# Attention, search, output projection and MLP of a hybrid trunk in two halves of the tokens

## The chip, the cores and the metric

The kernel runs on one core of one Trainium2 chip. Its engines are PE (TensorE, the matmuls, with PEld for their weight loads), DVE (VectorE), ACT (ScalarE), POOL (GpSimd) and SP (SyncE, which here only issues DMAs). Each engine takes its own instructions in order, and semaphores let them wait for each other. The metric is the device time of one execution in microseconds (us), the median of several.

## The reference

One transformer layer over 1,024 tokens of width 1,024, in float32:

```python
mod = silu(c) @ w_mod + b_mod                  # 6 vectors of 1,024: shift, scale, gate, twice
h = rmsnorm(x, g_attn) * (1 + sc1) + sh1
proj = h @ w_in                                # 1,024 -> 3,272 columns
o_a = stick_breaking_attention(q_a, k_a, v_a)  # 8 heads of 64, strictly causal
score = sum_j relu(q_idx_j . k_idx) * w_idx_j  # indexer, 8 heads; admissible: chunks of 64
_, idx = top_k(score, 256)                     # for each token
o_b = softmax(q . kv[idx] + bias) . kv[idx] . w_uv   # DSA attention, 8 heads, one latent of 128
o = concat(rmsnorm(o_a), rmsnorm(o_b))
x = x + ga1 * (o @ w_out)
h = rmsnorm(x, g_mlp) * (1 + sc2) + sh2
x = x + ga2 * (relu(h @ w_up) ** 2 @ w_down)   # 1,024 -> 4,096 -> 1,024
out = rmsnorm(x, g_final)
```

Stick-breaking weights are sigmoid(z) times the product of 1 - sigmoid(z) over the later admissible keys. A token sees no later chunk, so its attention needs keys and values up to its own chunk only.

## The kernel before, in words

Tokens are cut into eight blocks of 128, b = 0 to 7; block b attends to 128(b+1) keys. Pairs of blocks are numbered i = 0 to 3. Each float32 matmul is made of three (or two) matmuls of float32r halves: an operand is split into a rounded high part (`hi`) and the rest (`lo`), and `mm3` (L177) adds hi·hi, hi·lo and lo·hi. A split of a weight tile costs a DMA from SP, a copy on ACT (L173) and a subtraction on POOL (L174); `load_split` does it.

The program runs in this order. (1) x is normalised and transposed, the modulation's first two vectors are computed, and the indexer's scores `sc[b]` are made for b = 2 to 7 (L245 to L468). (2) For four pairs of heads, `sb_project` makes queries and keys (`qe`, `qo`, `ke`, `ko` and low parts, for all tokens, kept in SBUF), and `sb_weights` and `sb_finish` do the stick-breaking attention for the pairs i in the order SBO: scores on PE, two sigmoids on ACT (L707, L708), a product scan on DVE (L709), a product on POOL (L711), then in `av_pair` transposes on PE (L621, L623), their split by ACT and DVE or POOL (L626 to L632), and the weighted sum on PE (L644). Beside it runs the search: `topk_step` finds the 256th largest score bit by bit in 32 steps, for blocks 2 to 6 by counts on DVE (L503, L529) and for block 7 by a sign count on ACT (L552), and `topk_mask` writes the masks `mk[b]`. `dq_half` projects the DSA queries and stores them to DRAM; `mod_piece` computes the rest of the modulation on DVE (L400, L402). (3) `ds_weights` and `ds_finish` do the DSA attention for all four pairs of blocks, head by head. (4) `out_tile` does the output projection (`wo`, with all of w_out split in SBUF), the second norm, and `h2_pair` transposes and splits its result. (5) In pools of its own the MLP runs in eight groups of four: `up` for both halves of the tokens from one split of the weights, then `dn` for all eight blocks.

The lists MS, DQ and TK and the offsets PRI set after which step of the attention how much of the other work is put into the program. The framework then orders the instructions of each engine at compile time: a list scheduler takes the instruction that comes first in the program (shifted by `early`) among those that it believes ready, and so moves later work into idle time, as far as the tiles' buffers allow. SBUF tiles share tagged pools of fixed numbers of buffers, PSUM has eight banks: z 4, tr 3, av 1 up to the MLP, then p1 4 and p2 4.

## Time and profile before

| | us |
|---|---|
| median of 3 runs | 1626.39 (1625.78 to 1627.17) |
| the profiled execution's own time | 1625.42 |
| its span, first to last instruction | 1623.6 |
| mean granted PE clock, of full | 0.948 |
| PE busy | 1468.8 |
| DVE busy | 990.5 |
| ACT busy | 667.6 |
| POOL busy | 567.5 |

An engine's busy time is the time in which at least one of its instructions ran. Matmuls overlap in the records, since each is followed by the next before its own end, so that PE's busy time is longer than the time that the same matmuls need when they follow each other closely.

### The profile page before, as it was taken

Reading aid. Unit: us, or ns where it says so; the run is one execution under the profiler, and the core shown is the slowest. Engines: PE = TensorE matmul, PEld = TensorE weight load, DVE = VectorE, ACT = ScalarE, POOL = GpSimd, SP = SyncE. Lnnn points to the kernel's source line nnn. Section 1 sums busy time; section 2 is a strip of 40 time slices with the busy share of each in tenths; the row PEclk is TensorE's granted clock in tenths of the full one; section 3 lists DMA queues with packets and bytes.
Section 4 is the critical chain, followed back from the end, with each engine's and each line's share of the span. In section 5 each row is a group of like instructions: output and inputs, shape, how many; then the busy total and the mean of one; then the engine's idle time right before and its main releaser. Section 6 shows DMA issues by size and latency. Waiting matters only on the chain.

```text
span 1623.6 us, 19672 instructions
## 1 busy us (share of the span) xinstructions
PE 1468.8 (90%) x7248; PEld 1213.9 (75%) x7248; DVE 990.5 (61%) x1842; ACT 667.6 (41%) x1258; POOL 567.5 (35%) x389
## 2 busy tenths in 40 slices
...
PEclk8999979888899879999999999999999999999999
...
GB/s 324 150 105 28 78 46 39 105 64 91 34 40 40 68 55 85 91 59 53 117 143 101 208 94 0 92 13 78 26 65 40 53 52 39 66 27 78 6 34 104
DMA packets 103232, 121.49 MB, mean 75 GB/s; under 512 B 7856, under 2 KB 75480, under 8 KB 103136
## 3 DMA queue, kind: packets, MB, share of 16 engines
...
q14 instruction: 39, 0.32, 0.1%
...
## 4 chain that ended last, share of the span: by engine, by line
PE 61%; DVE 27%; issue 4%; ACT 3%; DMA 3%; POOL 1%; SPq 0%; DVEq 0%; POOLq 0%; ACTq 0%
PE up L178 7%; PE up L180 7%; PE up L179 7%; PE dn L178 7%; PE dn L179 7%; PE dn L180 7%; DVE tk_jk L503 4%; DVE tk_jk L529 4%; DVE m L709 4%; DVE m2acc L402 2%; DMA wm<-in_w_mod_dram 2%; PE wo L178 2%; PE wo L179 1%; PE wo L180 1%; PE avd L644 1%
## 5 line engine op out<-in xcount | busy, mean ns | idle before, releaser
L174 POOL TENSOR_TENSOR wld<-wrd,whd 128x1024 fp32r<-128x1024 f32 x32 | 77.3, 2415 | 474.5 <-ACT whd L173 474.5
L1138 DVE TENSOR_TENSOR x<-dn,x 128x512 f32<-128x512 f32 x128 | 87.7, 691 | 206.7 <-PE dn L180 206.7
L1119 ACT ACTIVATE r<-up 128x512 f32<-128x512 f32 x64 | 37.8, 591 | 402.7 <-PE up L180 402.7
L178 PE MATMUL up<-h2h,whup 128*128 128x512 f32 x512 | 200.0, 391 | 3.2 <-ACT h2f L1020 3.2
L179 PE MATMUL up<-h2l,whup 128*128 128x512 f32 x512 | 199.7, 390 | 0.0
L180 PE MATMUL up<-h2h,wlup 128*128 128x512 f32 x512 | 199.7, 390 | 0.0
L179 PE MATMUL dn<-wld,uh 128*128 128x512 f32 x512 | 199.2, 389 | 0.0
L180 PE MATMUL dn<-whd,ul 128*128 128x512 f32 x512 | 199.2, 389 | 0.0
L178 PE MATMUL dn<-whd,uh 128*128 128x512 f32 x512 | 196.6, 389 | 0.0
L1120 DVE SCALAR_TENSOR_TENSOR r<-up,r 128x512 f32<-128x512 f32 x64 | 44.3, 692 | 196.7 <-ACT r L1119 196.7
L711 POOL TENSOR_TENSOR be<-be,m 128x895 f32<-128x895 f32 (+7 forms) x64 | 89.5, 1401 | 170.0 <-DVE m L709 114.8
L709 DVE TENSOR_TENSOR_SCAN m<-m 128x896 f32<-128x896 f32 (+7 forms) x64 | 98.7, 1548 | 27.7 <-ACT m L707 25.3
L178 PEld LDWEIGHTS up<-h2h,whup 128*128 128x128 f32 x512 | 96.5, 188 | 23.5 <-ACT h2f L1020 3.5
L179 PEld LDWEIGHTS up<-h2l,whup 128*128 128x128 f32 x512 | 96.5, 189 | 20.1
L180 PEld LDWEIGHTS up<-h2h,wlup 128*128 128x128 f32 x512 | 96.4, 188 | 20.1
L178 PEld LDWEIGHTS dn<-whd,uh 128*128 128x128 f32 x512 | 96.1, 188 | 20.0
L180 PEld LDWEIGHTS dn<-whd,ul 128*128 128x128 f32 x512 | 96.1, 188 | 20.0
L179 PEld LDWEIGHTS dn<-wld,uh 128*128 128x128 f32 x512 | 96.1, 188 | 19.9
L174 POOL TENSOR_TENSOR wlup<-wrup,whup 128x1024 fp32r<-128x1024 f32 x32 | 77.1, 2408 | 27.3 <-ACT whup L173 27.2
L160 DVE TENSOR_TENSOR ul<-r,uh 128x512 fp32r<-128x512 f32 x64 | 57.2, 894 | 44.7 <-ACT uh L159 44.7
L529 DVE TENSOR_SCALAR_CACHE_REDUCE tk_jk<-mk,tlo,above 128x384 bf16<-128x384 uint16 (+4 forms) x80 | 74.7, 933 | 2.0
L644 PE MATMUL avs<-wts,va 128*128 128x256 f32 (+1 forms) x320 | 56.5, 306 | 16.4 <-DVE ota L662 7.3
...
## 6 DMA issues: line engine op xcount, KB each, us to landing
...
```

Source lines behind the costliest of these rows:

```text
L160: (lo_eng or V).tensor_tensor(lo, src, hi.bitcast(F32), op=OP.subtract)
L174: (lo_eng or G).tensor_tensor(lo, raw, hi.bitcast(F32), op=OP.subtract)
L178: T.matmul(ps, ah, bh, start=start, stop=False)
L179: T.matmul(ps, ah, bl, start=False, stop=False)
L180: T.matmul(ps, al, bh, start=False, stop=stop)
L503: V.tensor_scalar(jk[:, :widths[b]], src or sc[b], t, 0.5 - TOPK, op0=op, op1=OP.add, accum_out=c)
L529: V.tensor_scalar(jk[:, :widths[b]], mk[b].bitcast(U16), tlo[:, j:j + 1], above[:, j:j + 1], op0=OP.is_ge, op1=OP.add, accum_out=cnt[0][:, ...
L644: T.matmul(dst, vv, rhs, start=kt == 0 and l == 0, stop=half and l == 1)
L709: V.tensor_tensor_scan(m[:, :n][:, ::-1], m[:, :n][:, ::-1], m[:, :n][:, ::-1], 1.0, op0=OP.mult, op1=OP.bypass)
L711: G.tensor_tensor(be[:, :n - 1], be[:, :n - 1], m[:, 1:n], op=OP.mult)
L1120: V.scalar_tensor_tensor(r, ps, 0.0, r, op0=OP.max, op1=OP.mult)
L1138: V.tensor_tensor(x1[tt][:, cs], ps, x1[tt][:, cs], op=OP.add)
```

## The change

The tokens are worked in two halves of 512, hf = 0 (blocks 0 to 3) and hf = 1 (blocks 4 to 7), from the attentions to the end of the MLP. The projections are still made for all tokens, but q, k and v of the second half go to DRAM (`qd`, `khd`, `kld`, `vd`; the stores are issued by ACT) and come back head by head in `sb_second`. The search has two DVE groups, blocks (2, 3) and (4, 5, 6), beside block 7 on ACT. The first part of the program does stick-breaking and DSA attention of half 0, then `out_half(0)`. After that `mlp_beside` yields the MLP of half 0 in 96 steps (32 `up`, 64 `dn`), which the program alternates with stick-breaking of half 1, the rest of the search, and DSA of half 1. Then come `out_half(1)` and the MLP of half 1 alone. The weights w_up, w_down and w_out are therefore loaded and split once per half. What is left of the modulation after the indexer moves from DVE to ACT and POOL. The SBUF tiles qk, kl and va become one pool `qk` of 14 tiles of 4 KB. PSUM is z 3, tr 2, av 1 and a new m 2, which serves the projections and the MLP of half 0.

```diff
...
-TKB = ((2, 3, 4, 5, 6), (7,))
-TK0 = 1
...
+DEPTH = 2
+BUFS = {"wkL": 4, "wkS": 6, "qk": 14, "wt": 3, "ot": 2, "ot2": 1, "z": 4, "tr": 3, "av": 1}
+PS2 = {"z": 3, "tr": 2, "av": 1, "m": 2}
 MI = [4, 0, 5, 0, 2, 0, 0, 5]
-MS = [2, 0, 1, 2, 2, 1, 1, 1, 1, 1, 0, 1, 1, 0, 0, 0, 0, 0, 0, 0, 0, 0, 0, 0, 0, 0, 0, 0, 0, 0, 0, 0]
-DQ = [1, 1, 1, 1, 1, 2, 0, 2, 0, 1, 1, 1, 0, 0, 0, 0, 0, 0, 0, 0, 0, 0, 0, 1, 0, 0, 1, 0, 1, 0, 1, 0]
-TK = [1, 1, 2, 1, 1, 2, 0, 2, 2, 1, 4, 0, 4, 0, 2, 0, 1, 2, 4, 3, 0, 0, 1, 0, 2, 1, 1, 1, 0, 0, 0, 3]
+MS = [2, 2, 2, 2, 2, 2, 2, 2, 1, 1, 1, 1, 1, 1, 1, 1]
+DQ = [0, 0, 0, 0, 0, 0, 0, 0, 0, 0, 0, 0, 1, 1, 1, 1]
+TK = [3, 3, 3, 3, 3, 3, 3, 3, 3, 3, 3, 2, 0, 0, 0, 0]
+TA = [2, 2, 2, 2, 2, 2, 2, 2, 2, 2, 2, 2, 2, 2, 2, 2]
+D0 = [0, 1, 1, 2]
+FILL_S, FILL_T = 4, 3
+FILL_D = [2] * 18
 DBG = {}
...
+        def mtile(name):
+            return pp.tile([P, 512], F32, tag="m", bufs=bf["m"], name=name)
...
         def pjtile(name):
-            return pp.tile([P, 512], F32, tag="tr", bufs=TRB, name=name)
+            return (mtile if "m" in bf else trtile)(name)
...
-                if k == 0:
-                    V.tensor_scalar(acc, raw[:, 0, :], ck, None, op0=OP.mult)
+                if "m" in bf:
+                    A.activation(acc if k == 0 else raw[u], raw[u], AF.Copy, scale=ck)
+                    if k:
+                        G.tensor_tensor(acc, acc, raw[u], op=OP.add)
+                elif k == 0:
...
+        def search(blocks):
...
+                    V.tensor_tensor(thr, thi, fb, op=OP.bitwise_or)
+            yield begin
+            for i in range(31, 15, -1):
+                yield lambda i=i: upper_step(i)
+            for i in range(15, -1, -1):
+                yield lambda i=i: lower_step(i)
...
-                stack_q(ps, slice(hf * 512, hf * 512 + 512), r["qe"], r["qo"])
...
+                stack_q(ps, slice(0, 512), q[:, 0:512], q[:, 512:])
+                if hf:
+                    A.dma_start(qd[pr], q.bitcast(F32))
...
-                for k, l, p0 in ((r["ke"], r["le"], 0), (r["ko"], r["lo"], 64)):
...
                     p1 = 64 - p0
                     own, twin = slice(p0, p0 + 64), slice(p1, p1 + 64)
-                    A.activation(k[own, cs], ps[own], AF.Copy)
...
-                     lambda: (start_k(), half_k(0)), lambda: half_k(1)]
+                    A.activation(kl[own, 0:512], ps[own], AF.Copy)
+                    V.tensor_tensor(kl[own, 512:], ps[own], kl[own, 0:512].bitcast(F32), op=OP.subtract)
+                    if hf == 0:
+                        A.dma_start(kl.bitcast(F32)[twin, :], kl.bitcast(F32)[own, :])
+                        r[n] = kl
+                    A.dma_start(khd[pr][own, cs], kl.bitcast(F32)[own, 0:512])
+                    A.dma_start(kld[pr][own, cs], kl.bitcast(F32)[own, 512:])
...
+        def sb_weights(h, i, q, k, l):
             ws = []
+            if i < 2:
+                both = big(f"be{h}_{i}")
             for b in (2 * i, 2 * i + 1):
                 n = widths[b]
-                be = wktile(f"be{h}_{b}", n)
+                be = both[:, (b % 2) * 512:] if i < 2 else big(f"be{h}_{b}")
...
+        def sb_second():
...
+            def load(h):
+                pr, own = h // 2, slice(64 * (h % 2), 64 * (h % 2) + 64)
+                q = bp.tile([P, 512], F32R, tag="wkS", bufs=bf["wkS"], name=f"q2_{h}")
+                SY.dma_start(q.bitcast(F32), qd[pr][:, (h % 2) * 512:(h % 2 + 1) * 512])
+                kl = []
+                for n, src in (("h", khd), ("l", kld)):
+                    k = qktile(f"k2{n}_{h}")
+                    for p0 in (0, 64):
+                        SY.dma_start(k.bitcast(F32)[p0:p0 + 64, :], src[pr][own, :])
+                    kl.append(k)
+                v = qktile(f"v2_{h}").rearrange("p (k d) -> p k d", d=P)
+                SY.dma_start(v.bitcast(F32), vd[h // 4].rearrange("p (k h d) -> p k h d", h=4, d=P)[:, :, h % 4, :])
+                r[h] = (q, *kl), [v[:, k, :] for k in range(NB)]
...
+            def step(h, i):
+                if i == 3:
+                    if h % 2 == 0:
+                        ots[h // 2, 1] = bp.tile([P, 512], F32, tag="ot", bufs=bf["ot"], name=f"otc{h // 2}")
+                    if h < 7:
+                        load(h + 1)
+                todo.append((h, i, sb_weights(h, i, *r[h][0]), r[h][1]))
+                if len(todo) > 1:
+                    sb_finish(*todo.pop(0))
...
+        def vb_group(g, hf):
+            hi, lo = load_split([P, 4, 64], w_uv[4 * g:4 * g + 4].rearrange("h r d -> r h d"), f"u{g}_{hf}")
...
+        def ds_load(h, hf):
             r = {}
-            r["ql"] = qktile(f"dql{h}")
...
-            SY.dma_start(raw, dqd[h])
-            r["qh"] = qktile(f"dqh{h}")
+            raw = wktile(f"dqr{h}_{hf}", 512)
...
+            r["qh"], r["ql"] = both[:, 0:512], both[:, 512:]
             split(r["qh"], r["ql"], raw, A, G)
             if h % 2 == 0:
...
+        def ds_steps(hf):
+            todo = []
+            r = [None]
+            def first():
+                vb_group(0, hf)
+                r[0] = ds_load(0, hf)
+            def step(h, i):
+                todo.append((h, i, ds_weights(h, i, r[0])))
+                if i % 2 == 0:
+                    r[0] = ds_load(h + 1, hf) if h < 7 else None
+                if h == 3 and i % 2 == 0:
+                    while todo:
+                        ds_finish(*todo.pop(0))
+                    vb_group(1, hf)
+                if len(todo) > DEPTH:
+                    ds_finish(*todo.pop(0))
+            yield first
+            for h in range(8):
+                for i in (2 * hf + 1, 2 * hf):
+                    yield lambda h=h, i=i: step(h, i)
+            yield lambda: [ds_finish(*t) for t in todo]
+        pctx1.close()
+        bf.update(PS2)
+        pp = pctx.enter_context(tc.tile_pool(name="psb", bufs=1, space=PSUM, reuse_waits="tile"))
         r, steps = sb_project(0)
...
+        def wo_piece(kt, ch, hf, gate):
+            cs = slice(ch * 512, ch * 512 + 512)
+            n = f"o{hf}_{kt}_{ch}"
+            both = qktile(f"wb{n}")
+            hi, lo = both[:, 0:512], both[:, 512:]
+            load_halves(hi, lo, w_out[kt * P:(kt + 1) * P, cs], n, (bp, "wkS", bf["wkS"]), gate[ch])
+            return hi, lo
...
+        def out_half(hf):
...
+            zs = [(mtile if t == 3 else ztile)(f"wo{hf}_{t}") for t in range(4)]
+            for kt in range(KT):
+                hi, lo = wo_piece(kt, 0, hf, gate)
+                for t in range(4):
+                    ts = slice(t * P, (t + 1) * P)
+                    mm3(zs[t], oh_[kt, hf][:, ts], ol_[kt, hf][:, ts], hi, lo, kt == 0, kt == KT - 1)
+            w = [wo_piece(kt, 1, hf, gate) for kt in range(KT)]
...
+            for t in range(4):
+                ts = slice(t * P, (t + 1) * P)
+                xt, tt = xts[t], 4 * hf + t
+                z = ztile(f"wp{hf}_{t}")
+                for kt in range(KT):
+                    mm3(z, oh_[kt, hf][:, ts], ol_[kt, hf][:, ts], *w[kt], kt == 0, kt == KT - 1)
+                V.tensor_tensor(xt[:, 512:], z, xt[:, 512:], op=OP.add)
+                A.dma_start(x1d[tt * P:(tt + 1) * P, :], xt)
...
+        def up_tile(ft, hf, ps, r, uh, ul, lo_eng=None):
+            wuh, wul = load_split([P, KT, P], wu[:, :, ft * P:(ft + 1) * P], f"up{ft}_{hf}")
+            for kt in range(KT):
...
+        def mlp_beside():
...
+            def wd_load(fg, f, ch):
+                ft = fg * FFG + f
+                cs = slice(ch * 512, ch * 512 + 512)
+                both = qktile(f"wd{ft}_{ch}")
+                wd[f, ch] = both[:, 0:512], both[:, 512:]
+                load_halves(*wd[f, ch], w_down[ft * P:(ft + 1) * P, cs], f"d{ft}_{ch}", (bp, "wkS", bf["wkS"]))
+            def up(fg, f):
+                ft = fg * FFG + f
+                uh[f], ul[f] = htile(f"uh{ft}"), htile(f"ul{ft}")
+                up_tile(ft, 0, mtile(f"up{ft}"), wktile(f"r{ft}", 512), uh[f], ul[f])
+                wd_load(fg, f, 0)
...
+            def dn(fg, t, ch):
+                ps = mtile(f"dn{fg}_{t}_{ch}")
+                ts = slice(t * P, (t + 1) * P)
+                cs = slice(ch * 512, ch * 512 + 512)
+                for f in range(FFG):
+                    mm3(ps, uh[f][:, ts], ul[f][:, ts], *wd[f, ch], f == 0, f == FFG - 1)
...
+                else:
+                    V.tensor_tensor(acc[t, ch], ps, acc[t, ch], op=OP.add)
+                if ch == 0:
+                    wd_load(fg, t, 1)
...
+                    V.tensor_tensor(acc[t, ch], acc[t, ch], gate[0][ch], op=OP.mult)
+                    G.tensor_tensor(acc[t, ch], acc[t, ch], x1, op=OP.add)
...
+            for fg in range(NG):
+                for f in range(FFG):
+                    yield lambda fg=fg, f=f: up(fg, f)
+                for ch in range(2):
+                    for t in range(4):
+                        yield lambda fg=fg, t=t, ch=ch: dn(fg, t, ch)
+        norm(0, 0)
+        norm(0, 1)
+        run(s1, 1)
+        out_half(0)
+        run(s1, 1)
+        m = mlp_beside()
+        for _ in range(13):
+            run(s1, 1)
+            run(tk, FILL_T)
+            run(ta, 2)
+            run(m, FILL_S)
+        run(tk, 99)
+        run(ta, 99)
+        d = ds_steps(1)
+        for k in range(18):
+            run(d, 1)
+            run(m, FILL_D[k])
+        norm(1, 0)
+        run(m, 200)
+        norm(1, 1)
+        out_half(1)
+        pctx.close()
...
+        def up_group(fg):
             for f in range(FFG):
                 ft = fg * FFG + f
-                wuh, wul = load_split([P, KT, P], wu[:, :, ft * P:(ft + 1) * P], f"up{ft}")
-                uh[f] = gp.tile([P, S], F32R, tag="g4", bufs=16, name=f"uh{ft}")
-                ul[f] = gp.tile([P, S], F32R, tag="g4", bufs=16, name=f"ul{ft}")
-                for hf in (1, 0):
-                    cs = slice(hf * 512, hf * 512 + 512)
-                    ps = ptile(f"up{ft}_{hf}")
-                    for kt in range(KT):
-                        mm3(ps, wuh[:, kt, :], wul[:, kt, :], h2h[kt, hf], h2l[kt, hf], kt == 0, kt == KT - 1)
-                    r = gp.tile([P, 512], F32, tag="sq", bufs=2, name=f"r{ft}_{hf}")
...
```

## Rows read from the trace of the kernel before

**Rows 1.** The page: busy us, share and instructions of each engine; granted clock by slices.
```profile
PE 1468.8 (90%) x7248; PEld 1213.9 (75%) x7248; DVE 990.5 (61%) x1842; ACT 667.6 (41%) x1258; POOL 567.5 (35%) x389
...
PEclk8999979888899879999999999999999999999999
```

**Rows 2.** Windows by stage: length, busy us and instructions of PE, PEld, DVE, ACT, POOL, clock.
```profile
0.00:150.00 150.00, 113.50 (x542) 90.53 (x543) 119.41 (x168) 96.32 (x167) 59.73 (x51) 0.89 0.52 161
150.00:450.00 300.00, 240.39 (x1155) 194.85 (x1155) 294.58 (x620) 147.24 (x286) 95.04 (x60) 0.86 0.22 64
450.00:640.00 190.00, 159.06 (x910) 136.13 (x909) 134.66 (x141) 97.33 (x205) 102.97 (x64) 0.89 0.20 59
640.00:800.00 160.00, 149.01 (x1056) 128.25 (x1055) 144.09 (x492) 137.65 (x298) 100.68 (x72) 1.00 0.22 73
800.00:920.00 120.00, 110.33 (x526) 87.87 (x525) 59.50 (x118) 39.94 (x83) 50.55 (x56) 0.96 0.38 125
920.00:1617.00 697.00, 696.50 (x3070) 576.28 (x3068) 236.63 (x305) 148.41 (x220) 157.59 (x85) 1.00 0.18 57
```

**Rows 3.** Groups by line, PE: operation, shape, count, busy us, mean ns, idle before.
```profile
L178 PE MATMUL up<-h2h,whup 128*128 128x512 f32 x512 | 200.0, 391 | 3.2 <-ACT h2f L1020 3.2
...
L644 PE MATMUL avs<-wts,va 128*128 128x256 f32 (+1 forms) x320 | 56.5, 306 | 16.4 <-DVE ota L662 7.3 <-DVE wts L632 7.1 <-POOL wts L630 1.5
...
L178 PE MATMUL dq<-hh,whdq 128*128 128x512 f32 x128 | 54.8, 428 | 5.9 <-DVE qo L371 3.9 <-ACT whdq L173 1.3 <-ACT wfs L629 0.4
...
L623 PE MATMUL trs<-ident,be 128*128 128x128 f32 x160 | 41.0, 308 | 2.7 <-POOL be L711 2.7
...
L178 PE MATMUL v<-whv,hh 128*128 128x256 f32 x128 | 37.2, 290 | 0.0
```

**Rows 4.** Timeline of PE in the DSA stage: start us, us, operation.
```profile
769.36 0.27 PE L621 MATMUL trd<-ident,dl 128*128 128x128 f32 x1
769.47 0.27 PE L623 MATMUL trd<-ident,dl 128*128 128x128 f32 x1
...
770.99 1.13 PE L644 MATMUL avd<-wtd,vb 128*128 128x256 f32 x8
```

**Rows 5.** Groups by line, PE, window 640 to 800 us.
```profile
L644 PE MATMUL avd<-wtd,vb 128*128 128x256 f32 (+1 forms) x280 | 41.8, 286 | 2.6 <-DVE otb L662 1.1 <-ACT wtd L626 1.0 <-DVE wtd L632 0.3
L178 PE MATMUL dz<-kvh,dqh 128*128 128x384 f32 (+4 forms) x94 | 37.8, 403 | 4.2 <-DVE dst L812 3.0 <-DVE dst L817 1.1
```

**Rows 6.** Groups by line, DVE: scan, both kinds of count, modulation.
```profile
L709 DVE TENSOR_TENSOR_SCAN m<-m 128x896 f32<-128x896 f32 (+7 forms) x64 | 98.7, 1548 | 27.7 <-ACT m L707 25.3 <-POOL kvst L149 2.1
...
L529 DVE TENSOR_SCALAR_CACHE_REDUCE tk_jk<-mk,tlo,above 128x384 bf16<-128x384 uint16 (+4 forms) x80 | 74.7, 933 | 2.0
L503 DVE TENSOR_SCALAR_CACHE_REDUCE tk_jk<-mk,thr 128x384 bf16<-128x384 bf16 (+4 forms) x80 | 69.9, 874 | 1.2
...
L402 DVE SCALAR_TENSOR_TENSOR m2acc<-m2raw,c_act,m2acc 128x512 f32<-128x512 f32 x56 | 52.2, 932 | 7.5 <-DMA m2raw<-in_w_mod_dram 7.0
```

**Rows 7.** Groups by line, the MLP's work on the other engines.
```profile
L1138 DVE TENSOR_TENSOR x<-dn,x 128x512 f32<-128x512 f32 x128 | 87.7, 691 | 206.7 <-PE dn L180 206.7
...
L174 POOL TENSOR_TENSOR wlup<-wrup,whup 128x1024 fp32r<-128x1024 f32 x32 | 77.1, 2408 | 27.3 <-ACT whup L173 27.2
...
L160 DVE TENSOR_TENSOR ul<-r,uh 128x512 fp32r<-128x512 f32 x64 | 57.2, 894 | 44.7 <-ACT uh L159 44.7
...
L1120 DVE SCALAR_TENSOR_TENSOR r<-up,r 128x512 f32<-128x512 f32 x64 | 44.3, 692 | 196.7 <-ACT r L1119 196.7
...
L1119 ACT ACTIVATE r<-up 128x512 f32<-128x512 f32 x64 | 37.8, 591 | 402.7 <-PE up L180 402.7
```

**Rows 8.** Timeline of SP: one DMA issue.
```profile
702.61 0.32 SPq L831 DMA_DIRECT2D o<-otb  x1
```

**Rows 9.** Groups by form, DVE: the same comparison on 512 and 384 elements.
```profile
L578 DVE TENSOR_SCALAR eq<-sc,thr 128x512 f32<-128x512 f32 x1 | 1.7, 1696 | 0.0
...
L578 DVE TENSOR_SCALAR eq<-sc,thr 128x384 f32<-128x384 f32 x1 | 0.4, 395 | 0.0
```

849 lines of the change are left out of this document (392 added, 457 removed).

## The prediction, as put on record

> **What bounds the kernel now.** I read the page's busy times and clock first [rows 1], then the windows by stage [rows 2], then the groups by line, to count matmuls [rows 3, 5], and two timelines for spacings [rows 4, 8]. The reader is to see that PE is the busiest engine, but that its 90% is no measure of what it could give: in the last stage 3,070 matmuls of 512 columns start in 697.0 us, 0.227 us each, although each is recorded as 390 ns [rows 2, 3]. I therefore count work in spacings: 0.227 us for 512 columns; 0.12 us for 256 (eight in 1.13 us, the last of which ends some 0.3 us after its start) and 0.11 us for a 128-column transpose (769.36 to 769.47) [rows 4].
>
> In these units the work by stage is as follows, counts from the code and from [rows 3].
> - Projections: three lines of `mm3` with 128 matmuls each for dq, 384; as many for q and k together and for the output projection; kv 48. So q, k, dq and kv are 816 x 0.227 = 185 us, v (256 columns) 384 x 0.12 = 46, the output projection 384 x 0.227 = 87.
> - Stick-breaking: scores of 36 block columns of 128, twice, 8 heads, 144 times 512 columns, 33 us and 3 for the masks; 288 transposes 32; 320 weighted sums 38. Together 106 us.
> - DSA: scores three times instead of twice, 49 us and 3; transposes 32; sums 38; its values 48 x 0.12 = 6. Together 128 us.
> - Norms, the second transposes and the indexer's last pieces after 150 us: about 23 us.
>
> So from 150 to 920 us, 575 us of work took 770, three quarters. It splits unevenly. Between 640 and 800 us [rows 2, 5] ran 94/96 of the DSA scores, 7/8 of its sums and transposes, its values, and some 18 us of others: 51 + 33 + 30 + 6 + 18 = 138 of 160 us, 0.86, with DVE and ACT at 0.9. From 800 to 920 us about 100 of 120 ran. What remains, 575 - 138 - 100 = 337 us, took the 490 us from 150 to 640: 0.69. There DVE is full for 300 us (294.6) with the search's counts (145 us in all), the scans (99) and the modulation (52) [rows 6], and the granted clock is 0.86 to 0.89. The MLP's stage is bound by PE alone: 0.997, DVE at a third [rows 2]. Nothing can be won there, and some 150 us stand idle between 150 and 640.
>
> **The change part by part.** The stages after it are called A (to 150 us), B (projections, both attentions of half 0), C (output projection of half 0), D (MLP of half 0 beside the attentions of half 1), E (output projection of half 1), F (MLP of half 1).
>
> A: the same operations, 150 us.
>
> B: all projections, 185 + 46 = 231 us of PE. Of the attentions, blocks 0 to 3 have 1 + 2 + 3 + 4 = 10 of 36 block columns, 28%: 30 us and 36 us. With 15 for the spill from A and the small matmuls, 312 us. DVE has 32 counting steps for blocks 2 and 3: from the counts by width, 896 of 3,200 elements, 40 us, some 45 with small operations, masks and lower halves to 85; 28% of the scans and a little more since they are short, 33; the splits and evictions of projections and attentions, about 95; block 7's small operations 15. That is near 230 us. The rest of the search, about 135 us, is allowed to fill DVE's idle time here. The bounds of B are the two rates above: 312/0.86 = 363 and 312/0.69 = 452. I take 400, rate 0.78: less DVE work must be done here than before, but the filling counts again stand in front of other operations on an engine that takes them in order, and PE has only two banks for projections and two for transposes.
>
> C and E: 192 matmuls each, 44 us, and the gaps of such a chain (norm, square, power on POOL, transposes, split), 20 us in the row of 800 to 920 us [rows 2]. In C stick-breaking of half 1 is ready to fill, so I take 12 (0 to 20): 56. In E the last eight steps of the MLP cover the norm but not the way to the first `up`: 64.
>
> D: the MLP of half 0 is 1,536 x 0.227 = 349 us, stick-breaking of half 1 76, DSA of half 1 92: 517 us of PE. Done one after the other at the rates of before they take 349 + 76/0.69 + 92/0.86 = 566; perfectly mixed 517 to 520. I take 550, between them and nearer the first. DVE needs there about 71 (scans), 22 and 36 (splits of weights), 55 (DSA's sums and others), 95 for the MLP (32 x (692 + 894) + 64 x 691 ns [rows 7]) and 25 of masks, gates and last rows: some 305 us, and up to 440 if no count was done early. Both fit in 550.
>
> F: 349 us and the tail of 7 [rows 2]: 357 with a slower last pair.
>
> What is added and hidden: w_up and w_down are split twice. On POOL 32 x 2.41 us more for each [rows 7], 154 us, and 17 for w_out; POOL then has some 800 us over the program, about 310 in D, half of it. If PE didn't cover it, the 154 us would be the price. ACT gains some 70 us likewise. About 19 pieces of modulation move from DVE, 37 halves of 932 ns [rows 6], 34 us less, to ACT and POOL, which have room in B. The two search groups add 64 small operations: below nothing, above a count's own 874 ns each, 56 us; I take 16 us, on DVE, and it is in the 85 and 135 us. The round trip adds 74 DMA issues on ACT; at 0.32 us each as on SP [rows 8] 24 us of ACT in B, which also waits there in its order for the DVE half of each split, and behind it wait the next sigmoids and evictions; above, 74 times 1 us more. This is one reason why I don't put B at 0.86. The loads on SP are asked for a head ahead; SP's queue carries them past the MLP's weights, and a head has some 20 us of D, so I cost them at nothing.
>
> Sum: 150 + 400 + 56 + 550 + 64 + 357 = 1577. Outside the span lie 1625.42 - 1623.6 = 1.8 us, and the median of the runs is 1.0 above the profiled execution: 1580 us. Best bounds: 150 + 363 + 46 + 518 + 54 + 356 + 3 = 1490. Worst by the same rates: 150 + 452 + 64 + 566 + 70 + 358 + 3 = 1663.
>
> **The rivals.**
> First, better mixing: the list scheduler moves MLP matmuls into every gap, and B runs like the DSA stage. 150 + 363 + 50 + 522 + 60 + 357 + 3 = 1505. For it speaks that all engines but PE are under two thirds in D; against it, that before only one stage reached 0.86.
>
> Second, the other side, slower: the MLP's two `m` banks. Before, PE never waited for an eviction, with eight banks: DVE waited 206.7 us for `dn` [rows 7]. A `dn` step is 12 x 0.227 = 2.7 us, and its bank must be emptied by one DVE operation (691 ns) before the second next step; an `up` step needs ACT and DVE (591 + 692), and a group's first `dn` needs the whole chain with two more operations, about 2.8 us, behind whatever scan (up to 2.4) or mask stands in DVE's queue. If each of the 96 steps loses 1.2 us beyond what I allow, D is 665 and the time 1695; it decides from (1626 - 1580)/96 = 0.48 us a step. For it speaks that DVE and PE both take work in a fixed order that was planned at compile time; against it, that attention matmuls can stand between the steps.
>
> Third, no gain: B at 0.69, since the second search group keeps DVE full as in 150 to 450 us. 452 for 400 gives 1632.
>
> Fourth, DVE and POOL in turns. The rows show a comparison on 512 elements of 1,696 ns, where one on 384 takes 395 [rows 9], so something held it for a microsecond; but between 150 and 450 us DVE was busy 294.6 and POOL 95.0 of 300 [rows 2], so 90 us of POOL at least ran beside DVE. If POOL's 230 added us (the splits' 171 and the modulation's share) held DVE or were held in one to two thirds of the cases, and half of that came to light on PE, it is 40 to 75 us: up to 1655. The Trainium skill, "SBUF — State Buffer", section "Who interferes with whom", says that the two share one pair of ports as an exclusive lock, taken by DVE operations with two SBUF inputs or in a two-port mode; it speaks against a change that gives POOL 40% more to do, while counts with an accumulator are exempt. By that rule the scans' neighbours and the `ul` splits would meet POOL most, in D; the trace agrees with such single delays, and shows none as a rule.
>
> **How the numbers follow.** The forecast, 1545 to 1622, has 0.45; better mixing, 1485 to 1545, 0.17; no gain 0.13; the banks 0.17; the turns 0.08. Of "no gain" half lies within 0.2%, about what this kernel's measurement can tell from no change, and a little of it is faster. Faster: 0.45 + 0.17 + 0.02 = 0.64; same 0.06; slower 0.30. The range of 8 in 10 leaves the quickest twentieth and the worst of the banks' case: 1500 to 1675. The forecast's own range is 1545 to 1622.
>
> **What would show it.** In the changed profile: PE clock near 1.0 from C on; `up` and `dn` in two stretches, the later one some 350 us long at 0.227 us a matmul; the first `up` at about 610 us; counts of blocks 4 to 6 before that. D shorter than 566 us proves the mixing. The prediction is wrong if PE waits on DVE L1138's successor in `dn` for over 50 us, if B reaches past 620 us, or if the second stretch of the MLP starts late because its weights do.

## The result, and the profile of the changed kernel

The changed kernel takes 1735.6 us (median of 4 runs, 1733.6 to 1737.2) against 1626.8 for the kernel before on the same chip: ratio 1.0665, 95% interval 1.0646 to 1.0684. The forecast was 1580, the range ended at 1675. It is slower by 109 us, and 156 us above the forecast.

From the page of the changed kernel: PE's busy time and the granted clock in 40 slices. They answer to [rows 1].

```profile
PE 1512.3 (87%) x7352; PEld 1240.1 (71%) x7352; DVE 1101.0 (63%) x1943; ACT 776.4 (45%) x1414; POOL 783.9 (45%) x516
...
PEclk8989888999998797998899999999998899999999
```

The span is cut at the marks of the forecast's stages: the last weighted sum of DSA's first half (558 us), the first `up` (665), the last `dn` (1297), the first `vp` of the second MLP half (1377). Windows of the changed kernel by these marks (columns as in [rows 2], the last two numbers are the DMA engines' busy share and GB/s), and two stretches inside them:

```profile
0.00:150.00 150.00, 109.29 (x497) 83.91 (x498) 116.98 (x170) 96.96 (x171) 61.30 (x51) 0.89 0.52 164
150.00:558.00 408.00, 357.50 (x1942) 299.88 (x1943) 248.05 (x645) 223.98 (x443) 156.35 (x120) 0.92 0.40 115
558.00:665.00 107.00, 80.29 (x328) 61.87 (x328) 57.21 (x68) 41.62 (x78) 47.44 (x40) 0.80 0.37 114
665.00:1297.00 632.00, 560.96 (x2821) 462.14 (x2820) 441.43 (x827) 282.00 (x531) 305.21 (x189) 0.95 0.27 81
1297.00:1377.00 80.00, 53.86 (x234) 43.41 (x234) 49.65 (x65) 26.74 (x50) 42.05 (x42) 0.83 0.49 170
1377.00:1735.00 358.00, 350.37 (x1537) 288.94 (x1536) 187.65 (x171) 105.12 (x144) 171.53 (x76) 0.99 0.30 93
300.00:550.00 250.00, 233.86 (x1338) 197.56 (x1336) 104.45 (x259) 131.89 (x278) 102.55 (x81) 0.97 0.39 114
700.00:900.00 200.00, 153.19 (x691) 121.67 (x691) 196.18 (x331) 77.70 (x150) 84.04 (x49) 0.92 0.28 79
```

So A is 150 (forecast 150), B 408 (400), C 106 (56), D 632 (550), E 80 (64), F 358 (357). Three stages are right to within 8 us; the miss is C +50, D +82, E +16. (C ends at 664.5, hence 106.)

The last two windows show where D's loss sits. From 300 to 550 us DVE is busy 104 us of 250; from 700 to 900 it is busy 196 of 200, and PE 153. Groups of the changed kernel by line in that second stretch, with PE's wait at the end of its line:

```profile
L533 DVE TENSOR_SCALAR_CACHE_REDUCE tk_jk<-mk,tlo,above 128x640 bf16<-128x640 uint16 (+2 forms) x48 | 51.3, 1068 | 1.1
L502 DVE TENSOR_SCALAR_CACHE_REDUCE tk_jk<-mk,thr 128x640 bf16<-128x640 bf16 (+2 forms) x36 | 36.3, 1008 | 0.9
...
L158 PE MATMUL dn<-wd,uh 128*128 128x512 f32 x68 | 31.0, 463 | 19.6 <-DVE r L1131 17.2 <-DVE acc L1173 2.4
```

The two lines of counts are 84 of the 96 counts of the second search (blocks 4 to 6). Twelve were done before 665 us; the forecast had all of them in B's idle time. A timeline from the same stretch, cut down, shows what they stand in front of (start, duration, instruction):

```profile
864.75 2.41 POOL L155 TENSOR_TENSOR wlup<-wrup,whup 128x1024 fp32r<-128x1024 f32 x1 [0.99 <-ACT whup L154]
...
865.47 1.07 DVE L533 TENSOR_SCALAR_CACHE_REDUCE tk_jk<-mk,tlo,above 128x768 bf16<-128x768 uint16 x1
...
867.10 2.01 POOL L723 TENSOR_TENSOR be<-be,m 128x1023 f32<-128x1023 f32 x1
...
867.84 1.30 DVE L535 TENSOR_SCALAR cnt<-cnt 128x3 f32<-128x3 f32 x1
...
869.06 1.32 POOL L155 TENSOR_TENSOR wd<-wrd,wd 128x512 fp32r<-128x512 f32 x1
...
869.17 1.22 DVE L536 SCALAR_TENSOR_TENSOR tlo<-cnt,tlo 128x3 f32<-128x3 f32 x1
...
870.43 0.94 DVE L533 TENSOR_SCALAR_CACHE_REDUCE tk_jk<-mk,tlo,above 128x640 bf16<-128x640 uint16 x1
...
871.41 1.07 DVE L533 TENSOR_SCALAR_CACHE_REDUCE tk_jk<-mk,tlo,above 128x768 bf16<-128x768 uint16 x1
...
872.41 0.69 DVE L1131 SCALAR_TENSOR_TENSOR r<-up,r 128x512 f32<-128x512 f32 x1
...
873.15 0.50 PE L158 MATMUL up<-h2h,whup 128*128 128x512 f32 x1 [2.55 <-DVE r L1131]
...
874.25 0.17 DVE L535 TENSOR_SCALAR cnt<-cnt 128x3 f32<-128x3 f32 x1
```

PE stands for 2.55 us for a bank that one 0.69 us operation empties, because that operation is behind two counts and two small operations in DVE's order. The two small ones take 1.30 and 1.22 us here, while POOL works; the next of their kind, at 874.25 us with POOL idle, takes 0.17 (more on this in the last section).

### The profile page after: what moved, and what is told of

Read it like the earlier page. It is cut to its first block, busy times and chain, and to the rows that moved or that the text cites. A ratio compares the mean times of both kernels' runs of the same rounds, so it can differ in the third digit from the quotient of the medians.

```text
span 1735.0 us, 20688 instructions
## 1 busy us (share of the span) xinstructions
PE 1512.3 (87%) x7352; PEld 1240.1 (71%) x7352; DVE 1101.0 (63%) x1943; ACT 776.4 (45%) x1414; POOL 783.9 (45%) x516
## 4 chain that ended last, share of the span: by engine, by line
PE 54%; DVE 21%; POOL 5%; DMA 4%; issue 4%; ACT 3%; ACTq 0%; SPq 0%; POOLq 0%; DVEq 0%
DVE tk_jk L502 4%; PE en L158 3%; PE en L159 3%; PE en L160 3%; DVE m L721 3%; PE vp L158 3%; PE vp L159 3%; PE vp L160 3%; DVE tk_jk L533 3%; PE up L158 2%; PE dn L158 2%; PE up L159 2%; PE up L160 2%; PE dn L159 2%; PE dn L160 2%
## 5 line engine op out<-in xcount | busy, mean ns | idle before, releaser
L155 POOL TENSOR_TENSOR wlup<-wrup,whup 128x1024 fp32r<-128x1024 f32 x64 | 164.5, 2572 | 116.8 <-ACT whup L154 106.8
L158 PE MATMUL dn<-wd,uh 128*128 128x512 f32 x256 | 108.0, 427 | 23.4 <-DVE r L1131 17.2
L721 DVE TENSOR_TENSOR_SCAN m<-m 128x384 f32<-128x384 f32 (+3 forms) x64 | 102.0, 1600 | 24.6 <-ACT m L719 24.3
L159 PE MATMUL dn<-wd,uh 128*128 128x512 f32 x256 | 106.2, 416 | 2.3 <-POOL wd L155 2.3
L160 PE MATMUL dn<-wd,ul 128*128 128x512 f32 x256 | 104.8, 410 | 1.7 <-DVE ul L137 1.7
L160 PE MATMUL up<-h2h,wlup 128*128 128x512 f32 x256 | 102.5, 401 | 0.0
L158 PE MATMUL vp<-h2h,whup 128*128 128x512 f32 x256 | 100.5, 392 | 0.0
L158 PE MATMUL en<-whe,vh 128*128 128x512 f32 x256 | 99.7, 390 | 0.7 <-DVE x1b L1259 0.7
L160 PE MATMUL vp<-h2h,wlup 128*128 128x512 f32 x256 | 100.2, 391 | 0.0
L159 PE MATMUL vp<-h2l,whup 128*128 128x512 f32 x256 | 100.2, 391 | 0.0
L159 PE MATMUL en<-wle,vh 128*128 128x512 f32 x256 | 99.6, 389 | 0.0
L160 PE MATMUL en<-whe,vl 128*128 128x512 f32 x256 | 98.8, 389 | 0.0
L153 DVE TENSOR_TENSOR wre<-wre,gate 128x1024 f32<-128x1024 f32 x32 | 76.7, 2396 | 18.3 <-DMA wre<-in_w_down_dram 18.2
```

Source lines behind the costliest of these rows:

```text
L153: V.tensor_tensor(raw, raw, scale, op=OP.mult)
L155: (lo_eng or G).tensor_tensor(lo, raw, hi.bitcast(F32), op=OP.subtract)
L158: T.matmul(ps, ah, bh, start=start, stop=False)
L159: T.matmul(ps, ah, bl, start=False, stop=False)
L160: T.matmul(ps, al, bh, start=False, stop=stop)
L721: V.tensor_tensor_scan(m[:, :n][:, ::-1], m[:, :n][:, ::-1], m[:, :n][:, ::-1], 1.0, op0=OP.mult, op1=OP.bypass)
```

## The experiments

All stages of all runs, in us, cut at the same marks. A is 150 everywhere. The ratio is to the kernel before on the same chip, with its 95% interval.

| run | B | C | D | E | F | median us | ratio |
|---|---|---|---|---|---|---|---|
| forecast | 400 | 56 | 550 | 64 | 357 | 1580 | |
| changed kernel | 408 | 106 | 632 | 80 | 358 | 1735.6 | 1.0665 (1.0646 to 1.0684) |
| e1_mask_last | 455 | 106 | 573 | 81 | 359 | 1727.4 | 1.0611 (1.0594 to 1.0628) |
| e2_no_second_search | 397 | 107 | 571 | 80 | 359 | 1667.7 | 1.0255 (1.0232 to 1.0277) |
| e3_third_bank | 411 | 108 | 627 | 90 | 358 | 1745.5 | 1.0724 (1.0708 to 1.0740) |
| e4_gate_at_sum | 405 | 99 | 633 | 78 | 357 | 1726.5 | 1.0609 (1.0585 to 1.0632) |
| e5_counts_spread | 442 | 106 | 569 | 82 | 358 | 1710.1 | 1.0529 (1.0510 to 1.0549) |
| e56_rows_elsewhere | 437 | 102 | 575 | 81 | 365 | 1713.9 | 1.0555 (1.0527 to 1.0583) |
| e56c_fill_first_projection | 442 | 177 | 528 | 82 | 365 | 1744.0 | 1.0733 (1.0716 to 1.0750) |
| e57_mlp_tail_last | 445 | 106 | D and E 647 | | 363 | 1711.6 | 1.0530 (1.0513 to 1.0546) |
| e8_counts_thin | 410 | 114 | 605 | 81 | 359 | 1719.6 | 1.0557 (1.0526 to 1.0587) |
| e89_dq_earlier | 438 | 109 | 603 | 80 | 358 | 1740.6 | 1.0692 (1.0663 to 1.0720) |
| e84_thin_gate_at_sum | 411 | 106 | 604 | 78 | 360 | 1711.8 | 1.0514 (1.0483 to 1.0546) |
| e11_pieces_split_before | 428 | 98 | 607 | 62 | 360 | 1707.6 | 1.0489 (1.0465 to 1.0513) |
| e2_11_no_counts_no_pieces | 424 | 99 | 581 | 63 | 358 | 1674.9 | 1.0284 (1.0248 to 1.0319) |
| e5_11_spread_pieces | 464 | 93 | 575 | 62 | 358 | 1705.0 | 1.0479 (1.0457 to 1.0501) |
| e12_11_block6_on_scalare | 433 | 102 | 592 | 64 | 360 | 1702.6 | 1.0459 (1.0435 to 1.0484) |
| e15_projection_undisturbed | 400 | 74 | 645 | 83 | 358 | 1710.0 | 1.0506 (1.0478 to 1.0534) |
| e16_all_together | 441 | 74 | 594 | 78 | 360 | 1701.7 | 1.0457 (1.0426 to 1.0487) |
| e13_attention_then_mlp | 458 | in the text | | 87 | 357 | 1838.4 | 1.1297 (1.1272 to 1.1322) |

### Where the counts went

The first theory came from the code. Every count writes its unused output into one tile (tag `jk`, one buffer), tiles of a tag are given out in program order, and `run(ta, 2)` in the MLP's loop issues the mask of block 7 as its first thing, ahead of most of the second search. The rows on the tile `thr` of the changed kernel (first and last start at the end) agree: block 7's threshold stands at 287.5 us, its mask starts at 692.9.

```profile
L574 DVE TENSOR_SCALAR thr<-thr x1: 154/154/154, 287.5 to 287.5; 128x1 f32<-128x1 f32 x1
L575 DVE TENSOR_SCALAR nq<-sc,thr x1: 753/753/753, 692.9 to 692.9; 128x1024 f32<-128x1024 f32 x1
```

**e1_mask_last**

```
             run(s1, 1)
             run(tk, FILL_T)
-            run(ta, 2)
             run(m, FILL_S)
```

> One line goes: the mask of block 7 is no longer written into the MLP's loop but after the second search. First theory, the order of one 2 KB tile: every count of the search writes its unused result into one single tile, and such tiles are given out in program order. The mask of block 7 stands in that order ahead of all but the first three steps of the second search, and needs 4 KB tiles that are not free before the output projection is done; so the counts of blocks 4 to 6 can't move into the 60% idle time of VectorE between 300 and 550 us, and fill VectorE from 700 to 900 us, where PE does 131 us of work in 200. Then this run has those counts before 550 us, VectorE under 60% between 700 and 900, the MLP stage beside the attentions (668 to 1290 us now, 622 us) at 550 to 570 us, and 1660 to 1690 us in all. Second theory, the two banks of the MLP and the hand-over of its steps: the stage stays above 605 us and the time above 1715. Third, the counts are as much in the way before 550 us as later: the stage shortens, but the projections' stage grows by as much, 1725 to 1745.

**e2_no_second_search** (the counts of blocks 4 to 6 are left out; their masks use a threshold of zero)

```
-        tk, ta = chain(*[search(g) for g in GROUPS]), search_act(ACT_BLOCK)
+        tk, ta = chain(search(GROUPS[0]), search_none(GROUPS[1])), search_act(ACT_BLOCK)
```

> Leaves out the counts of the second search (blocks 4 to 6 get a mask with a threshold of zero), all else as in the changed kernel, the mask of block 7 in its place. It measures what those counts cost wherever they stand. First theory (their pile-up between 700 and 900 us): the MLP stage falls from 622 to 545 to 570 us and the time to 1655 to 1685. Second theory (banks and hand-over): the stage stays above 600 us, the time above 1710. If the run is well below the one with the mask moved, the counts cost something before 550 us too.

The windows 300 to 550 and 700 to 900 us of e1_mask_last, then the MLP stage of e2_no_second_search:

```profile
300.00:550.00 250.00, 207.90 (x1095) 172.41 (x1094) 188.73 (x432) 105.21 (x218) 89.04 (x70) 0.90 0.29 87
700.00:900.00 200.00, 185.50 (x927) 153.05 (x928) 104.73 (x111) 110.56 (x214) 126.44 (x75) 0.93 0.41 115
```

```profile
654.00:1225.00 571.00, 541.34 (x2823) 450.91 (x2821) 320.47 (x571) 282.59 (x532) 314.45 (x189) 0.98 0.30 90
```

One line moved the counts, as the first theory said: DVE from 300 to 550 us goes from 104 to 189 us, D from 632 to 573. But B pays 47 us for it, and the whole gains 8. All counts together cost 68 us (1735.6 - 1667.7) in the place that the change gave them, and 60 in e1's. So the first theory is right on where the loss of D comes from and wrong on what could be had; the third, "as much in the way before 550 us", holds. Of the 61 us between D with and without counts, 41 are idle time of PE (632 - 561 against 571 - 541), the other 20 its longer busy time at a lower granted clock (0.95 against 0.98).

**e3_third_bank**

```
-PS2 = {"z": 3, "tr": 2, "av": 1, "m": 2}
+PS2 = {"z": 2, "tr": 2, "av": 1, "m": 3}
...
-            zs = [(mtile if t == 3 else ztile)(f"wo{hf}_{t}") for t in range(4)]
+            zs = [(mtile if t >= 2 else ztile)(f"wo{hf}_{t}") for t in range(4)]
```

> The MLP gets a third PSUM bank and the scores one less (2 for 3). Second theory (two banks: a step must be emptied before the second next): PE waits less for the MLP's evictions, the stage of 622 us loses 30 to 60 us, 1675 to 1705 us. First theory (a full VectorE in order): the evictions are late by more than a bank can cover, and scores lose a bank: 1725 to 1750 us.

It is 10 us slower (E 90, D 627), as the first theory had it; the scores' lost bank is in that. Waits of PE in D, of the changed kernel and then of this run (total us, times, longest):

```profile
PE dn L158 <- DVE r L1131: 17.2, 6, 6.7
PE avs L660 <- DVE wts L648: 15.9, 10, 3.4
PE up L158 <- DVE r L1131: 8.4, 5, 2.6
PE dn L158 <- DVE acc L1173: 6.1, 5, 2.1
```

```profile
PE dn L158 <- ACT uh L136: 9.1, 2, 7.6
PE dn L160 <- DVE ul L137: 8.6, 5, 3.9
...
PE dn L158 <- DVE r L1131: 4.4, 4, 2.6
```

L1131 is the last operation that reads an `up` bank and L1173 the one that empties a `dn` bank, so in the changed kernel PE waits 32 us in D for the MLP's two banks (17.2 + 8.4 + 6.1). With three, `dn` waits 4 us for L1131 and 18 for its split inputs, which come later in the same order of DVE. And with two banks but without the counts, in e2, the waits for the banks are 6 us. So more banks don't help an eviction that stands behind counts.

**e5_counts_spread**, two search steps behind each eviction of a dq projection, held there by one copied element:

```
                 A.activation(f, ps, AF.Copy, scale=P ** -0.5)
+                jk = mp.tile([P, S], BF16, tag="jk", bufs=1, name=f"tk_jt{h}_{hf}")
+                V.tensor_copy(jk[0:1, 0:1], f[0:1, 0:1])
+                run(tk, 2)
```

with e1's line left out too.

> The mask of block 7 comes after the search as in the run that moved it, and two steps of the second search follow each of the 16 evictions of a dq projection; one copied element of that eviction, written into the search's single 2 KB tile, keeps them from being taken earlier. Before: moving the mask alone took 59 us off the MLP stage (632 to 573, from the first up to the last dn) and put 47 on the projections' (408 to 455), and the counts together cost 68 us wherever they stood, as the run without them showed. Theory of the bunch: the counts cost PE because some 25 us-long stretches of them stand back to back on an engine that takes its work in order; two steps (some 5 us) in each 10 us, where VectorE is idle for 60%, cost little: projections' stage 408 to 420, MLP stage 570 to 580, 1670 to 1690 us in all. Rival: every count is in front of something, so the price is the same anywhere: 1718 to 1735 us.

**e8_counts_thin**, one step at a time, in three stages (`count_after` is the copy and `run(tk, n)` of above):

```
                 ws.append(l)
+            if i < 2:
+                count_after(ws[-1], 1)
...
                 A.dma_start(x1d[tt * P:(tt + 1) * P, :], xt)
+                if hf == 0:
+                    count_after(xt, 1)
...
+                r = wktile(f"r{ft}", 512)
+                up_tile(ft, 0, mtile(f"up{ft}"), r, uh[f], ul[f])
+                count_after(r, 1)
```

> The second search one step (three counts, 4.4 us of VectorE) at a time, each behind a copied element of something late: 16 in the DSA of the first half (400 to 560 us), 4 in the first output projection, the rest behind one up step of the MLP each. The run with two steps behind each dq eviction still paid 42 us for the counts (1710 against 1668 without them), 34 of them in the projections' stage, where VectorE was full from 400 to 600 us. Theory of the bunch: one step in 10 us leaves VectorE idle between them, the projections' stage is 410 to 425 us, the first projection's 106 to 112, the MLP's 575 to 590: 1675 to 1695. Rival, each step costs its price wherever it stands: 1705 to 1730.

Spread counts cost 42 us, thin ones 52. The 16 steps that stand one per DSA step add 13 us to B (410 against 397 without counts), so bunching is part of the price; but the 12 steps left for the MLP's stage cost 34 us there (605 against 571), 2.8 us each for 4.9 us of DVE (379 us busy in the stage against 320). Unbunching takes off 26 of the 68 us at best, not the whole; both theories that put these runs at 1670 to 1695 were wrong, e8 lies in its rival's range and e5 below its own.

**e89_dq_earlier**

```
-DQ = [0, 0, 0, 0, 0, 0, 0, 0, 0, 0, 0, 0, 1, 1, 1, 1]
+DQ = [2, 0, 2, 0, 2, 0, 2, 0, 2, 0, 0, 0, 2, 0, 2, 0]
```

> The thin counts, and the dq projections no longer all behind the others (from 380 us on) but a head's two at every second step of the first attention, in the stretch from 200 to 300 us where PE does 31 us of work in 50 because VectorE is full of the first search. dq needs no VectorE. Theory (the projections' stage loses its time to what VectorE holds up, and PE has nothing else there): the stage of 408 us falls by 20 to 40 us, the rest as in the run with the thin counts. Rival: the two banks of the projections are given out in order, so that a dq step stands behind one whose bank waits for VectorE: within 8 us of the thin counts alone.

Neither: 21 us more. PE did take the work earlier (the last dq at 498 us, not 539), but then DSA and its thin counts stood alone at the end of B (from 500 to 560 us DVE is busy 58.8 us and PE 41.8, in e8 42.9 and 53.1), and the stage grew from 410 to 438. The dq matmuls had been the filler of that stretch.

### Whether the mixing is worth anything

**e13_attention_then_mlp** (based on e1's order of the mask)

```
-            run(ta, 2)
-            run(m, FILL_S)
...
             run(d, 1)
-            run(m, FILL_D[k])
+        run(m, 200)
         norm(1, 0)
-        run(m, 200)
```

> The mixing undone and nothing else: stick-breaking of the second half with the second search, then its DSA, and only then the MLP of the first half, all in the order of the program. One after the other at the rates of before I had 566 us for the three, mixed 550, and measured 632 with the counts in it and 571 without. If the mixing is worth what it seemed (PE takes MLP work where the attention waits): the stage from the first norm's end to the last dn is 80 to 130 us longer (counts and scans alone need 250 us of VectorE, DSA 110, the MLP 350), 1800 to 1860 us in all. If the mixing gives back what it wins by standing in VectorE's order: within 25 us of 1736.

Windows of this run, from the end of the first output projection to the first `up`, and from there to the last `dn`:

```profile
701.00:943.00 242.00, 164.36 (x842) 131.72 (x842) 169.99 (x256) 127.47 (x263) 98.66 (x68) 0.74 0.21 58
943.00:1392.00 449.00, 428.68 (x1991) 345.16 (x1990) 166.11 (x330) 161.57 (x273) 207.24 (x125) 0.99 0.29 89
```

The kernel with the mask moved and everything mixed takes 1727.4, this one 1838.4: the mixing is worth at least 111 us. At least, since the scheduler still put most of the DSA beside the MLP: 160 of its 224 weighted sums lie in the second window. Done nearly one after the other, the three parts take 691 us where the prediction had 566. The size that it had wrong is stick-breaking's: alone, and with no counts left to do (the last starts at 449.7 us), it and the rest of the DSA take 242 us at a granted clock of 0.74 with PE busy 68%, where the prediction's rate of 0.69 gave 110 for all of stick-breaking.

### The two projection stages

**e4_gate_at_sum**

```
-            load_halves(hi, lo, w_out[kt * P:(kt + 1) * P, cs], n, (bp, "wkS", bf["wkS"]), gate[ch])
+            load_halves(hi, lo, w_out[kt * P:(kt + 1) * P, cs], n, (bp, "wkS", bf["wkS"]))
...
+                V.tensor_tensor(g, z, gate[ch], op=OP.mult)
+                V.tensor_tensor(dst, g, dst, op=OP.add)
```

> In the two output projections the gate is no longer multiplied into the 16 pieces of the weights but into the 8 sums, as one more operation each. It is for the 115 and 90 us of the two projection stages (56 and 64 foretold). Theory of the pieces: each piece goes load, gate on VectorE, copy on ScalarE, difference on GpSimd through two free 2 KB tiles, 2.6 + 0.7 + 0.6 + 1.3 us and the waits between, one piece per 3 us; and the loads wait for the two gate tiles, which wait for the same small tiles. Without the gate the first piece comes some 15 us earlier and pieces follow every 2.2 us: the first stage falls by 15 to 30 us, the second by 5 to 15, 1690 to 1715 us in all. Rival: what holds the stage is that nothing of it can begin before the attentions of the first half free their tiles (548 to 583 us, PE at a third), and the way behind the last sum (norm, transposes, split); then the time falls by less than 10 us.

9 us, just the rival's side: C 99, E 78. **e84_thin_gate_at_sum** is the same edit on e8.

> The thin counts and the gate at the sums of the output projections. Alone the gate gave 9 us (7 in the first projection's stage, 2 in the second's). If the two are independent: 9 us less than the thin counts alone, 5 to 14. If the gate's gain came from VectorE in the MLP stage's pile-up: 0 to 4.

8 us less than e8 (C 106 for 114, E 78 for 81): independent of the counts.

**e11_pieces_split_before**, on top of e84; one call for each of the 16 steps of the first attention, and the projections load `wod`:

```
+        def wo_split(kt, ch):
+            both = big(f"ws{kt}_{ch}", F32R)
+            load_halves(both[:, 0:512], both[:, 512:], w_out[kt * P:(kt + 1) * P, ch * 512:ch * 512 + 512], f"o{kt}_{ch}", (bp, "wkS", bf["wkS"]))
+            A.dma_start(wod[kt, ch], both.bitcast(F32))
```

> The thin counts, the gate at the sums, and w_out split once, piece by piece during the first attention, both halves of each piece written to DRAM; the two output projections load them ready made, without the 2 KB tiles, ScalarE and GpSimd. It takes the chain of the pieces out of both projection stages (106 and 80 us). Theory of the pieces: the first sum starts some 15 us after the last weighted sum of the first half, in place of 36, and the stage falls to 70 to 85 us, the second to 62 to 72: 25 to 45 us less than with the gate alone. Rival, the chain of norms, transposes and free 4 KB tiles sets both stages: within 10 us of the run with the gate at the sums, or more, if 16 pieces more on ScalarE and GpSimd hold up the attention: the projections' stage then grows by 10 to 20.

4 us less than e84: which the runs' spread can't tell from nothing (1705.9 to 1709.0 against 1707.2 to 1715.5). By stages E falls to 62 as the theory of the pieces had it, C only to 98, and B grows by 17: the rival, within 10 us, holds for the sum. The second projection stage of this run:

```profile
1282.00:1344.00 62.00, 45.83 (x205) 36.87 (x203) 31.53 (x51) 16.07 (x31) 15.57 (x24) 0.86 0.53 199
```

So E was long because of its pieces, C for the most part was not, and the split costs in B most of what it gives.

**e56_rows_elsewhere** (x rows in idle tiles of the weights' pool, on e5) and **e56c_fill_first_projection** (eight steps of stick-breaking inside the projection):

```
-                xt = big(f"xr{hf}_{t}")
+                xt = wp.tile([P, S], F32, tag=("wh", "wl")[t // 2], bufs=2, name=f"xr{hf}_{t}")
```

```
+                fill()
+                fill()
                 if t % 2:
                     h2_pair(2 * hf + t // 2, xts[t - 1:t + 1])
...
-        out_half(0)
+        out_half(0, lambda: run(s1, 1))
```

> The spread counts, and the rows of x of the output projections no longer in the four 4 KB tiles that stick-breaking uses too, but in tiles of the weights' pool, idle there. Theory of the shared tiles (stick-breaking of the second half was to fill the output projection's stage, but the four x rows hold all four of its tiles from 590 us until the norm): the stage of 106 us keeps its length or loses up to 10, but stick-breaking steps run in it; 10 to 20 us less than with spread counts alone. Rival (the stage's own chain sets it, and the scores have no PSUM bank in it, since the sums hold three of three): within 6 us of it.

> As the run with the rows elsewhere, and two of the four sums in the MLP's banks, so that one bank is left for scores, and eight steps of stick-breaking written into the second part of the first output projection; the MLP's steps are dealt over the fewer steps that remain beside it. Theory of the shared tiles and banks: the 60 us in which PE stands in that stage take up to 38 us of scores, transposes and sums, the MLP stage falls by 20 to 35 us, 20 to 35 us less than with spread counts alone. Rival, DVE, ScalarE and GpSimd are then as late for the projection's own pieces as they were idle: the stage grows by what the MLP stage loses, within 8 us of spread counts alone.

The first gives nothing (1713.9 against 1710.1), the rival's case. The second went past both expectations: D falls by 41, more than its theory had, but C grows by 71. That was the hint: in C the filler is the trouble.

**e15_projection_undisturbed**, on the changed kernel

```
-        run(s1, 3)
+        run(s1, 1)
...
         norm(0, 1)
-        run(s1, 1)
         out_half(0)
-        run(s1, 1)
...
-        for _ in range(13):
-            run(s1, 1)
+        for k in range(13):
+            run(s1, 2 if k < 4 else 1)
```

> The changed kernel, and no stick-breaking of the second half ahead of or in the first output projection: its first four steps go into the MLP's loop (two a turn there at first). It was to fill that stage; the trace shows scans, products and sigmoids of it between 565 and 597 us, and the loads of the gates, of the x rows and of the first pieces of w_out waiting for its tiles (first piece asked for at 583 us, 25 after the last weighted sum). If the filler is what lengthens the stage: the first sum starts 15 to 25 us after the last weighted sum for 36, the stage is 72 to 88 for 106; the MLP stage gets 19 us of PE work more, which it does partly beside: 1705 to 1728 us in all. If the stage's own chain of norm, pieces and transposes sets it: 98 or more, and 1738 to 1755.

SP's timeline in this stage, of the changed kernel first, then of this run; between them what SP waited for in the changed kernel from 556 to 630 us:

```profile
562.21 15.69 SPq L1025 DMA_DIRECT2D gate<-gate  x2
583.52 0.33 SPq L151 DMA_DIRECT2D wro<-in_w_out_dram  x1
...
590.06 0.33 SPq L151 DMA_DIRECT2D wro<-in_w_out_dram  x1
...
596.33 31.72 SPq L151 DMA_DIRECT2D wro<-in_w_out_dram  x14
```

```profile
SPq L1025 <- PE sz L363: 15.1, 1, 15.1
SPq L151 <- POOL wts L646: 6.3, 2, 5.5
SPq L1095 <- PE trs L639: 5.1, 1, 5.1
...
SPq L1095 <- POOL be L723: 4.2, 1, 4.2
```

```profile
548.12 1.36 SPq L1025 DMA_DIRECT2D gate<-gate  x2
549.52 35.43 SPq L151 DMA_DIRECT2D wro<-in_w_out_dram  x16
```

```profile
150.00:550.00 400.00, 353.46 (x1941) 296.71 (x1940) 248.53 (x646) 223.73 (x443) 157.40 (x121) 0.94 0.39 116
550.00:625.00 75.00, 58.66 (x245) 47.40 (x246) 42.48 (x54) 26.10 (x45) 36.13 (x31) 0.84 0.39 121
625.00:1269.00 644.00, 571.91 (x2901) 471.80 (x2902) 460.20 (x839) 296.26 (x563) 323.88 (x197) 0.95 0.29 85
```

In the changed kernel all four waits end with an operation of stick-breaking (scores `sz`, transposes `trs`, `wts`, `be`), which lets go of the tile that the gate, the first piece or a row of x is loaded into. With stick-breaking kept out, the gates and the first piece are asked for at the end of the attention and not 25 us after it, the first sum starts 10 us after the last weighted sum (before, 35), C is 74 and the kernel 25.6 us faster, although D takes the four steps back with 13 us.

**e57_mlp_tail_last** (`run(m, 200)` behind `out_half(1)`, on e5)

> The spread counts, and in the second output projection's stage (80 us, foretold 64) the last steps of the MLP are written after the projection, so that they can fill its gaps instead of going ahead of it. Theory: PE waits there because the pieces of the weights get their small tiles only after the MLP's last rows (x1, y) have left them; with the order turned the first piece is loaded earlier and the eight steps of 2.7 us fill the gaps before the projection and before the next up: 10 to 22 us less than with spread counts alone. Rival: the two gates and the pieces still get no tile earlier and the chain stays: within 5 us, or up to 10 us more, since the MLP of the second half can't begin until the last rows are out.

Within 2 us of e5: the projection does start earlier (1247 us for 1284), and the last `dn` ends 79 us later (1345 for 1266), just before the second MLP half begins; D and E together are 647 for 651.

### Together

**e2_11_no_counts_no_pieces** joins the edits of e2 and e11 (again without the counts of blocks 4 to 6), **e5_11_spread_pieces** those of e5 and e11.

> Leaves out the counts of the second search (a threshold of zero for blocks 4 to 6), and has the pieces of w_out split before and the gate at the sums. Alone the counts were worth 68 us and, beside thin counts, pieces and gate together 12 (projection stages 114 to 98 and 81 to 62, but 18 more in the stage in which they are split). If the terms are independent: projections' stage 400 to 415, first projection's 92 to 100, MLP's 565 to 575, second projection's 60 to 65: 1640 to 1655 us, still above the kernel before; what is missing to the forecast then lies in the first projection's stage (40 us), in the MLP's (20) and in the projections' (10). If the MLP stage or the first projection's shrinks too (below 550, below 80), they waited for what was left out.

> Two steps of the second search behind each dq eviction (1710 us) with the gate at the sums and the pieces of w_out split before. The second projection's stage has 62 for 82, the first's 98 for 106, and 10 to 18 come back on the projections' stage: 1692 to 1706 us. It is the best order of the counts together with the best of the pieces. If the split of the pieces meets the counts on VectorE and GpSimd: 1706 to 1720.

Without counts the pieces are no gain at all (1674.9 against 1667.7: B +27, C -8, D +10, E -17), with spread counts 5 us. The terms are not independent: work put into B lengthens B.

**e12_11_block6_on_scalare**, on e11 (`run(ta, 2)` also goes beside each DSA step of the first half)

```
-GROUPS = ((2, 3), (4, 5, 6))
+GROUPS = ((2, 3), (4, 5))
...
-        tk, ta = chain(*[search(g) for g in GROUPS]), search_act(ACT_BLOCK)
+        tk, ta = chain(*[search(g) for g in GROUPS]), chain(search_act(ACT_BLOCK), search_act(6))
```

> The thin counts with the pieces split before (1708 us), and block 6, the widest of the second search, searched on ScalarE as block 7 is, after it: 32 signs with a sum and 64 small operations for VectorE in place of 32 counts of 896 elements. VectorE loses some 25 us of counts and gets 64 small operations of 0.15 us and more. Theory of VectorE's order (what stands in its queue is what PE waits for): the MLP stage of 607 falls by 10 to 25, 1680 to 1698 us in all. Rival: the small operations are as much in the way as the counts, or ScalarE gets late for the scores: 1700 to 1725.

D falls by 15, as the theory had it, but B and C take back 9 and E 2; 5 us less in all, inside the rival's range.

**e16_all_together** (e5, e4, block 6 on ScalarE, e15)

> What helped, together: two steps of the second search behind each dq eviction, block 6 on ScalarE, the gate at the sums, the first output projection undisturbed. Singly they gave 26, about 5 (beside other edits), 9 and what the undisturbed projection gives. If they add up: 1670 to 1695. If they meet in VectorE's order before 550 us: 1695 to 1715. No theory brings it below the 1627 of the kernel before.

1701.7, no clearer than e12's 1702.6, and 4.6% slower than the kernel before. C keeps its 74 us, but B is 441 and D 594 (569 in e5): the gains don't add up.

## Why the prediction was wrong, point by point

**A** and **F** came within 1 us. **B**'s 408 for 400 is luck: the 400, at the assumed mean of two rates, had the counts of blocks 4 to 6 in it, and the changed kernel did 12 of those 96 there. With the counts where the forecast put them (e1) B is 455, just past its worst bound of 452; without any (e2) it is 397. The costs of [rows 7]: the sums (L1173) 687 ns, as before; the split of w_up 2,572 ns where it took 2,408; w_down's gate 2,396 ns where it took 1,226 in the kernel before. None of it shows in F, where PE covers it. (The last stage's busy share is 0.999 by [rows 2], not 0.997; nothing hangs on it.)

```profile
L1173 DVE TENSOR_TENSOR acc<-dn,acc 128x512 f32<-128x512 f32 x56 | 38.1, 687 | 43.8 <-PE dn L160 43.8
```

```profile
L155 POOL TENSOR_TENSOR wlup<-wrup,whup 128x1024 fp32r<-128x1024 f32 x64 | 164.5, 2572 | 116.8 <-ACT whup L154 106.8
...
L153 DVE TENSOR_TENSOR wre<-wre,gate 128x1024 f32<-128x1024 f32 x32 | 76.7, 2396 | 18.3 <-DMA wre<-in_w_down_dram 18.2
```

**D: the step that failed is one sentence of B**, "The rest of the search, about 135 us, is allowed to fill DVE's idle time here". Nothing in the data forbids it; the order of a single scratch tile does, through the mask of a block that had been searched 400 us earlier. And the step left next to nothing for these counts: between B's 363 at the best rate and the 400 taken lie 37 us, which B without any of them used up (397). The fallback, "up to 440 if no count was done early. Both fit in 550", summed DVE over the stage. DVE's sum was exact (441 us), but the program deals the steps of the search over the turns of stick-breaking, ahead of the DSA that reads its masks, so they fell into 200 us, where DVE was full. That makes 61 of D's 82 us, and the runs say more: the work was never hideable for nothing, since no order brought its price below 42 us. The other 21 (571 without any count) are the term itself: its "one after the other" bound of 566 was far off (691), by 76/0.69 for stick-breaking, so that mixing gains at least 111 us where I had 16, and still doesn't reach 550. What makes up the 21 no run took apart.

**C: "In C stick-breaking of half 1 is ready to fill, so I take 12"** had the sign wrong. The filler holds the 2 KB and 4 KB tiles that the projection's loads wait for (SP's waits above), and its own operations stand on the engines that make the projection's splits. Together this is 32 of the 50 us, shown by leaving the filler out of the stage; the two were not told apart, except that moving the 4 KB rows of x alone gained nothing (e56). Some 18 us more than foretold remain in the undisturbed stage; its own chain of norm, pieces and transposes is what is left there, but no run took it apart.

**E**: the pieces of w_out had no term. With them ready E is 62 for 64 foretold, so the missing term is their way through load, gate, copy and difference: 18 us, of which the gate is 2 (e4). In the changed kernel the first sum of E starts 17 us after the last `dn`, so that the MLP's last steps cover nothing of it; in e11 it starts 19 us before.

**The rivals.** The banks' D was nearer than mine, 632 for its 665, and PE did wait 32 us for the two banks. But a third bank only moved those waits, and without the counts two banks cost 6 us (e3, e2). What is right in it is the queue of DVE behind which an eviction stands. "No gain" put the loss into B, which had none; its 452, with DVE full of the second search, is what e1 measured (455). The turns of DVE and POOL occur and are part of D's loss (below), 14 us of DVE's time in its small operations alone. They aren't what makes the counts dear: in e1 the same operations stand in B and take 0.24 us on average (0.61 in the changed kernel), and the counts still cost 60 us. What the turns cost in all no run took apart; taking the gate from the pieces gave 9 us. Better mixing didn't happen.

**The tests that I named**: first `up` at 665 us for 610; twelve counts of blocks 4 to 6 before it, not all 96; D above 566; the granted clock near 1.0 from C on: 0.80 in C, 0.95 in D, 0.83 in E, 0.99 in F. Each failed and pointed at the right stages. The later stretch of the MLP did take 358 us for some 350. PE's wait on the sums alone (over 50 us foretold for the banks) was 6, but the banks' other wait, on `up`'s last reader, was 26. B did not reach past 620 us.
